# A price for changing the division of the PE array in a kernel's instruction planner

## The chip, the cores and the metric

One core of a Trainium2 chip runs the whole kernel. Its engines are TensorE (PE, the matrix engine with an array of 128 x 128), VectorE (DVE), ScalarE (ACT), GpSimd (POOL) and SyncE (SP, which issues most DMAs). The metric is the device time of one execution in microseconds. Before the change three runs took 1368.52 us in the median (1365.78 to 1373.71).

## The reference

One inference step of a network of two layers, width 1024, on 384 tokens: 128 context tokens and 256 latent tokens with caches of 128 more. Weights are shared by both groups of tokens; all data is float32. A layer is, in the reference's words cut to what matters:

```python
h = rmsnorm(x, norm1_g) * (1 + sc1) + sh1      # sh, sc, g of six: silu(c) @ w_mod + b_mod
z = split_cols(h @ w_in)                       # inputs of A, B, C, D and four gates
oa = gqa_attention(aq, ak_all, av_all)         # A: 4 heads of 64, q/k norm, rotary
ob = gla_bidir(bq, bk, bv, lg_f, lg_b, ...)    # B: gated linear attention, both ways, key width 32
oc = diff_attention(cq, ck_all, cv_all, lam)   # C: 4 heads, two softmaxes of width 32 subtracted
od = gqa_attention(dq, dk_full, dv_all)        # D: low-rank keys and values, 4 heads of 96
x = x + g1 * (sum(sigmoid(gate_j) * (o_j @ w_branch_j)) @ w_out)
h = rmsnorm(x, norm2_g) * (1 + sc2) + sh2
x = x + g2 * ((gelu(conv3(h @ w_ffu)) * (h @ w_ffg)) @ w_ffd)
```

After two layers there is a last norm, and the context tokens' keys, values and states of every layer are outputs too.

## The kernel before

**Dense work.** A weight tile of 128 rows comes by DMA into one of three raw buffers, is cast on ACT into a high part (wh), and DVE subtracts to get the low part (wl); there are three buffers of each. Activations are kept in two parts as well (hh, hl; act_h, act_l), and each product is three matmuls in float32r: high by high, high by low, low by high. This is the stream called main: it walks through 260 weight tiles in a fixed order. In a layer these are the inputs of A and D (zA, zD), of C (zC, zV), of B (bqk, zB); then for each of the branches A, D, C, B eight tiles of gate and branch projection; then the output projection, the FFN's up projection (function ffn_up and the ones before it) and its down projection (ffn_down: eight output tiles of three weight tiles each, 66 matmuls of 384 columns).

**Small work.** Four mixers run beside main as streams of their own (mixer_a to mixer_d), and so does the modulation of later phases (mods): DVE multiplies a row of w_mod by the conditioning value and adds it to an accumulator, 8 rows for each half of a group and for 2 conditioning vectors; finish (line 450) then sums over the partitions with a list of eight matmuls that have 32 weight columns, transposes, and adds the bias. The next half waits until finish's list has been issued. Groups (layer, which of six): (0,2), (0,3), (0,4) in the mixers of layer 0; (0,5), (1,0), (1,1), (1,2) in its FFN; (1,3), (1,4) in the mixers of layer 1; (1,5) in its FFN. A group has two halves. The residual after the down projection of layer 0 (resid, line 1368) holds its PSUM bank until (0,5), (1,1) and (1,0) are done.

**The planner.** All streams are Python generators, and the class Sched merges them into the engines' programs when the kernel is built. It keeps an estimated clock for each engine (self.t), made of prices for each instruction (Op.price; a dense matmul of 384 columns counts 163 ns). In each step run() takes, of all streams that offer an instruction or a list of instructions, the one with the smallest rank: the start in whole ns, then the priority, then the order of creation.

```python
t = max(t, self.t[op.eng] + (1283.0 if self.swap(op) else 0.0))
...
return t // Q, s.prio(), s.seq
```

The first line is in start() (line 165) and is followed by the times at which inputs are ready and outputs free; the last is rank()'s (line 177). emit() (line 183) puts one instruction into its engine's program and moves the clock; every instruction of the kernel is issued in line 208, so the profile has that line throughout. Priorities (line 45): finish 0, A 1, D 2, C 4, B 6, the modulation's DVE work 6, main 9; the smaller wins. A stream that waits for a condition or a buffer offers nothing until it has it.

**Places where main waits.** For a weight tile (getw); for a PSUM bank of kind D (three of them, while the mixers have four of kind M and the modulation and the norms share one of kind X); in the last input tile of B (zB) for the end of A (line 1268); in the first tile of each branch (branch, line 1322) for the end of its mixer; at the end of a phase for the streams of that phase.

**Divisions of the array.** By rows used of the array and columns of weights, rounded up to 32, 64 or 128: dense matmuls, most transposes and the scores of C and D (96 rows) are 128 x 128. A's scores are 64 x 128 (64 rows), the value products of A and D and D's keys 128 x 64, B's gate inputs 64 x 128 (33 rows), B's far levels 32 x 128, B's near levels and finish 128 x 32.

Of the kernel before, what the change touches and what calls it, by code (L numbers as in the profile page):

```python
# [48 lines left out]
MS = (0, 5), (1, 0), (1, 1), (1, 2), (1, 3), (1, 4), (1, 5)  # L49
MG = ((0, 2), (0, 3), (0, 4)), MS[:MN[0]], MS[MN[0]:MN[1]], MS[MN[1]:]  # L50
TICK = 3413.0
WIN, THIN = 4500.0, 0.3
RC = (0.6127977038364543, -2.043313830363309, 1.8766171890415242)

# [2 lines left out]


class Op:
    """One instruction, made now and put into its engine's program later."""  # L60

    def __init__(self, eng, fn, f, args, kw):
        aps = [(k, v) for k, v in list(enumerate(args)) + list(kw.items()) if isinstance(v, bass.AP)]
        self.eng, self.fn, self.f, self.args, self.kw = eng, fn, f, args, kw
        self.outs = [v for k, v in aps if k in (0, "out", "accum_out")]
        self.ins = [v for k, v in aps if k not in (0, "out", "accum_out")]
        self.cost = self.price()
        self.func = TABLES.get(args[2]) if fn == "activation" else None
        self.rows = self.ins[0].shape[0] / 128 if eng == "P" else 0
        self.thin = self.rows == 0.25  # L70
        if self.rows and self.outs[0].free_size() == 2:
            self.rows = 0.02

# [33 lines left out]


class Slots:
    """Buffers of one kind, handed out and given back by the streams."""  # L110

    def __init__(self, sched, pool, tags, shape):
        self.sched, self.pool, self.free, self.shape = sched, pool, list(tags), shape
# [27 lines left out]


class Sched:
    """Merges streams of instructions into the engines' programs: of the streams' next instructions the one that can
    start first by the engines' estimated clocks is put in, ties by priority. A stream yields an instruction, a list
    of instructions that stay together, a condition to wait for, or a buffer it asks for."""

    LAT = dict(zip("PVS", LATS))

    def __init__(self):  # L150
        self.t = dict(P=0.0, V=0.0, S=0.0, G=0.0, D=0.0, Q=0.0)
        self.ready, self.touch, self.table = {}, {}, "none"
        self.live, self.seq, self.groups, self.thin = [], 0, Counter(), Counter()
        self.duty = Counter()

# [9 lines left out]
    def start(self, ops):  # L165
        t = 0.0
        for op in ops:
            t = max(t, self.t[op.eng] + (1283.0 if self.swap(op) else 0.0))
            for v in op.ins:
                t = max(t, self.ready.get(v.name, 0.0))  # L170
            for v in op.outs:
                for e, x in self.touch.get(v.name, {}).items():
                    if e != op.eng:
                        t = max(t, x)
        return t
# [7 lines left out]
    def emit(self, op):  # L183
        b = self.start([op])
        if op.eng == "P":
            i = b // TICK
            cost = op.cost * (1 if self.duty[i - 1] > 0.375 * TICK else 2)
            self.duty[i] += min(cost, (i + 1) * TICK - b) * op.rows
            self.duty[i + 1] += max(0.0, b + cost - (i + 1) * TICK) * op.rows
        else:  # L190
            cost = op.cost
        e = self.t[op.eng] = b + cost
        if self.swap(op):
            self.table = op.func[:2]
        if op.thin:
            self.thin[b // WIN] += cost
        if op.fn == "dma_start":
            n = op.outs[0]
            q = max(e + 650, self.t["Q"])
            e = self.t["Q"] = q + n.shape[0] * n.free_size() * 4 / 360.0  # L200
            d = e + 900
        else:
            d = e + self.LAT.get(op.eng, 130.0)
        for v in op.outs:
            self.ready[v.name] = d
        for v in op.ins + op.outs:
            self.touch.setdefault(v.name, {})[op.eng] = d
        op.f(*op.args, **op.kw)  # L208
# [46 lines left out]
def trunk_kernel(es, tc, a, o):  # L255
# [79 lines left out]
    def mm(out, lhsT, rhs, start, stop):  # L335
        return PE.matmul(out, lhsT=lhsT, rhs=rhs, start=start, stop=stop)
# [1 line left out]
    def tr(out, x):  # L338
        return PE.transpose(out, x, ident)

    # weights: load, split into two parts of float32r, use

    st = dict(dma=0, use=0, want=-1)
    ready = {}
# [71 lines left out]
        yield from prod()  # L416
        yield V.scalar_tensor_tensor(y, t, 1.5, y, op0=ALU.add, op1=ALU.mult)

    # modulation

    def mod_setup():
        cv = C("cvec").rearrange("p (k m) -> p k m", k=8)
# [65 lines left out]
        yield has(("acc",) + todo[-1][:3])  # L488
        pool.release(*acc)

    # norms

    def bcast(ph, y, want):
        b = yield X.ask()
# [146 lines left out]
            else:  # L641
                yield S.activation(dst[:, s:e], dst[:, s:e], AF.Identity, scale=scale, bias=sh[:, m:m + 1])

    # mixers

    def rope(z, h, n, cos, sin):
        half = n // 4
# [585 lines left out]
        done.difference_update([("acc", h) for h in range(4)])  # L1233
        done.add(("B", l))

    # dense parts

    def evac(env, name, t, p, bank, n, l):
        z = env[name]
# [236 lines left out]

        return [([(a["wfd%d" % i][l, d], 128 * FD[i])], lambda d=d, i=i: part(d, i)) for d in range(8) for i in range(len(FD))]

    # phases

    mx = fp = None

# [362 lines left out]
```

## Time and profile before

| | before |
|---|---|
| median of three runs | 1368.52 us |
| span of the profiled execution | 1371.2 us |
| PE busy | 1352.2 us, 8230 matmuls |
| DVE busy | 1025.2 us |
| ACT busy | 674.7 us |
| mean granted clock of PE | 0.988 |

The profile is one execution of its own, with a span from the first to the last instruction. Busy times are unions of instructions; matmuls are pipelined, so the duration that a row gives for one is longer than the distance to the next, and a distance is read from the starts. Names are those of tiles, out <- in, without buffer numbers: d, m and x are PSUM banks, mr and sq the modulation's buffers, kT, q, k, e of the attention mixers, pk, s, zD, rt of B.

### The profile page before, as it was taken

The page shows a single profiled execution, that of the slowest core. Times are in us where ns is not written, and L with a number is a line of the kernel's source. Part 1 is how long each engine was busy: PE and PEld are TensorE (multiplying, and loading weights), DVE is VectorE, ACT ScalarE, POOL GpSimd, SP SyncE. Part 2 cuts the span into 40 slices and gives each one's busy share as a digit, 9 for nine tenths or more (in the row PEclk, how much of TensorE's full clock was granted, in tenths as well). Part 3 has the DMA queues.
Part 4 walks back from the last instruction along what each step waited for, and adds up shares of the span by engine and source line. Part 5 has one row for each costly group of instructions (what it writes and reads, how often), then busy time and mean ns, then how long its engine had stood idle before and what let it go on. Part 6 is the DMA issues. An engine that isn't in the chain of part 4 may idle for free. (4 is left out here: it accounts for less than half of the span.)

```text
span 1371.2 us, 22142 instructions
## 1 busy us (share of the span) xinstructions
PE 1352.2 (99%) x8230; PEld 1249.9 (91%) x8230; DVE 1025.2 (75%) x2141; ACT 674.7 (49%) x1298; POOL 27.3 (2%) x55
## 2 busy tenths in 40 slices
PE   8999999999999999999999999999999999999996
PEld 5786799889999999999998668889999999999996
DVE  5699799876578999997479897786556889655433
ACT  4545665664366444433354566764344654444321
POOL 0000000100000000000001000100000000000000
PEclk8999999999999999999999998999999999999998
DMA  9754764223435566665447445222344365333331
GB/s 361 243 185 125 217 204 157 81 97 121 143 117 184 181 204 207 201 213 177 138 139 242 144 163 166 75 97 97 119 146 133 106 214 171 123 123 121 123 127 60
DMA packets 77084, 214.13 MB, mean 156 GB/s; under 512 B 9616, under 2 KB 17104, under 8 KB 76976
## 3 DMA queue, kind: packets, MB, share of 16 engines
q1 hardware_dynamic: 74592, 206.71, 45.9%
q0 software_dynamic: 2384, 6.00, 1.3%
q8 instruction: 65, 1.06, 0.3%
q14 instruction: 43, 0.35, 0.1%
HBM read 204.78 MB, written 7.90 MB: 155 GB/s over the span
## 5 line engine op out<-in xcount | busy, mean ns | idle before, releaser
L208 ACT CAST wh<-raw 128x1024 fp32r<-128x1024 f32 (+3 forms) x260 | 277.9, 1069 | 270.2 <-PE d L208 179.8
L208 PE MATMUL d<-hl,wh 128*128 128x384 f32 (+1 forms) x1184 | 405.4, 342 | 0.0
L208 PE MATMUL d<-hh,wl 128*128 128x384 f32 (+1 forms) x1184 | 405.4, 342 | 0.0
L208 PE MATMUL d<-hh,wh 128*128 128x384 f32 (+1 forms) x1184 | 401.7, 339 | 0.0
L208 DVE TENSOR_TENSOR wl<-raw,wh 128x1024 fp32r<-128x1024 f32 (+3 forms) x260 | 324.1, 1247 | 97.9 <-ACT wh L208 93.4
L208 PEld LDWEIGHTS d<-hh,wl 128*128 128x128 f32 x1184 | 223.6, 189 | 4.1 <-issue 3.6
L208 PEld LDWEIGHTS d<-hl,wh 128*128 128x128 f32 x1184 | 223.8, 189 | 3.4 <-issue 2.9
L208 PEld LDWEIGHTS d<-hh,wh 128*128 128x128 f32 x1184 | 223.6, 189 | 2.8 <-issue 2.4
L208 PE MATMUL d<-act_l,wh 128*128 128x384 f32 x352 | 119.4, 339 | 0.0
L208 PE MATMUL d<-act_h,wl 128*128 128x384 f32 x352 | 119.3, 339 | 0.0
L208 PE MATMUL d<-act_h,wh 128*128 128x384 f32 x352 | 119.2, 339 | 0.0
L208 DVE SCALAR_TENSOR_TENSOR sq<-sq,cact,sq 128x512 f32<-128x512 f32 x140 | 101.1, 743 | 3.5 <-DMA sq<-wmod_in 3.5
L208 DVE SCALAR_TENSOR_TENSOR mr<-mr,cact,mr 128x512 f32<-128x512 f32 x140 | 100.8, 744 | 1.9 <-DMA mr<-wmod_in 1.9
L208 ACT ACTIVATE gt<-d 128x384 f32<-128x384 f32 x64 | 31.4, 490 | 102.1 <-PE d L208 101.9
L208 DVE SCALAR_TENSOR_TENSOR fc<-d,vec,fc 128x255 f32<-128x255 f32 (+1 forms) x152 | 61.6, 411 | 26.4 <-ACT fc L208 25.7
L208 DVE SCALAR_TENSOR_TENSOR gt<-gt,d 128x384 f32<-128x384 f32 x48 | 26.6, 554 | 71.1 <-PE d L208 64.1
L208 PE MATMUL d<-wh,hh 128*128 128x512 f32 (+2 forms) x192 | 72.0, 375 | 1.0 <-DVE zC L208 1.0
L208 PE MATMUL d<-wh,hl 128*128 128x512 f32 (+2 forms) x192 | 70.9, 369 | 0.0
L208 PE MATMUL d<-wl,hh 128*128 128x512 f32 (+2 forms) x192 | 70.7, 368 | 0.0
L208 PEld LDWEIGHTS d<-act_l,wh 128*128 128x128 f32 x352 | 66.1, 188 | 0.3 <-issue 0.2
L208 PEld LDWEIGHTS d<-act_h,wl 128*128 128x128 f32 x352 | 66.1, 188 | 0.2 <-issue 0.2
L208 PEld LDWEIGHTS d<-act_h,wh 128*128 128x128 f32 x352 | 66.1, 188 | 0.2 <-issue 0.2
(321 smaller groups left out, 2076.5 us busy)
## 6 DMA issues: line engine op xcount, KB each, us to landing
raw<-wgb_in SPq DMA_DIRECT2D x64, 640.0 KB, 3.9
raw<-wf_in SPq DMA_DIRECT2D x72, 512.0 KB, 3.5
sq<-wmod_in SPq DMA_DIRECT2D x80, 256.0 KB, 3.3
mr<-wmod_in SPq DMA_DIRECT2D x80, 256.0 KB, 3.3
raw<-wfd_in SPq DMA_DIRECT2D x32, 448.0 KB, 3.3
raw<-wo_in SPq DMA_DIRECT2D x16, 512.0 KB, 3.5
raw<-wfd_in SPq DMA_DIRECT2D x16, 512.0 KB, 3.5
raw<-wf_in SPq DMA_DIRECT2D x16, 384.0 KB, 2.9
```

Of the source, the lines that this page charges most:

```text
L208: op.f(*op.args, **op.kw)
```

## The change

Each PE instruction gets a mode, the division of the array that it needs. The planner keeps the mode of the last PE instruction that it issued, and start() adds 95 ns for every PE instruction whose mode is another.

```diff
+SWITCH = 95.0
...
     def __init__(self, eng, fn, f, args, kw):
...
+        self.mode = tuple(32 if n <= 32 else 64 if n <= 64 else 128 for n in (self.ins[0].shape[0], self.ins[0].free_size())) if eng == "P" else None
...
     def __init__(self):
...
+        self.mode = (128, 128)
...
         for op in ops:
             t = max(t, self.t[op.eng] + (1283.0 if self.swap(op) else 0.0))
+            if op.eng == "P" and op.mode != self.mode:
+                t += SWITCH
...
     def emit(self, op):
         b = self.start([op])
         if op.eng == "P":
+            self.mode = op.mode
```

The first operand of a matmul is its weights (lhsT), so the mode is (rows, weight columns). Nothing else changes but comments: no instruction is added or taken away, only their order on the engines may be another.

## Rows read from the trace of the kernel before

**Rows 1.** The page: busy time of the engines; PE's granted clock in 40 slices

```profile
PE 1352.2 (99%) x8230; PEld 1249.9 (91%) x8230; DVE 1025.2 (75%) x2141; ACT 674.7 (49%) x1298; POOL 27.3 (2%) x55
...
PEclk8999999999999999999999998999999999999998
```

**Rows 2.** Waits of PE: who for whom, us in total, times, longest

```profile
PE m L208 <- DMA pk<-wmp_in: 3.8, 1, 3.8
...
PE d L208 <- DVE zC L208: 1.0, 3, 0.4
```

**Rows 3.** The page's costliest groups: busy, mean ns | idle before, releaser

```profile
L208 ACT CAST wh<-raw 128x1024 fp32r<-128x1024 f32 (+3 forms) x260 | 277.9, 1069 | 270.2 <-PE d L208 179.8
```

**Rows 4.** Timeline of PE around one small list: start, us, instruction

```profile
301.60 0.34 PE L208 MATMUL d<-hh,wh 128*128 128x384 f32 x1
301.87 0.43 PE L208 MATMUL m<-pk,s 128*32 128x128 f32 x8
302.23 0.44 PE L208 MATMUL d<-hh,wl 128*128 128x384 f32 x1
302.50 0.34 PE L208 MATMUL d<-hl,wh 128*128 128x384 f32 x1
302.68 0.33 PE L208 MATMUL d<-hh,wh 128*128 128x384 f32 x1
```

**Rows 5.** Timeline of PE: the first and the last small run of 119

```profile
11.11 1.08 PE L208 MATMUL m<-pk,oc 128*32 128x256 f32 x8 [3.80 <-DMA pk<-wmp_in]
...
1168.04 0.65 PE L208 MATMUL x<-mr,cst 128*32 128x128 f32 x16
```

**Rows 6.** Timeline of PE in the first FFN

```profile
473.50 0.64 PE L208 MATMUL x<-mr,cst 128*32 128x128 f32 x16
...
597.70 0.34 PE L208 MATMUL d<-act_h,wh 128*128 128x384 f32 x1
```

**Rows 7.** Stretches: length, busy PE, PEld, DVE, ACT, POOL, clock, DMA

```profile
249.00:329.00 80.00, 80.00 (x576) 71.25 (x575) 61.94 (x134) 49.34 (x110) 3.95 (x8) 1.00 0.26 90
...
416.00:597.00 181.00, 181.00 (x1097) 178.60 (x1096) 168.91 (x305) 84.64 (x129) 0.00 (x0) 1.00 0.62 199
```

**Rows 8.** Tile mr: durations min/median/max, first and last start

```profile
L208 DVE SCALAR_TENSOR_TENSOR mr<-mr,cact,mr x140: 736/745/752, 437.6 to 1166.3; 128x512 f32<-128x512 f32 x140
...
L208 DVE TENSOR_SCALAR mr<-mr,cact x20: 475/480/490, 436.1 to 1145.4; 128x512 f32<-128x512 f32 x20
```

**Rows 9.** Timeline of PE: A, then D, then B in layer 0

```profile
94.02 2.65 PE L208 MATMUL m<-kT,q 64*128 64x128 f32 x10
...
117.59 0.61 PE L208 MATMUL m<-e,zA 128*64 128x128 f32 x8
...
124.50 1.07 PE L208 MATMUL m<-kT,pk 128*64 128x512 f32 x2
...
155.29 0.88 PE L208 MATMUL m<-e,s 128*64 128x128 f32 x12
...
328.01 0.49 PE L208 MATMUL m<-cs,k 128*128 128x128 f32 x3
```

**Rows 10.** Same stretch, tile wh (PE, PEld, DVE, ACT), tile gt (DVE, ACT)

```profile
249.00:329.00 80.00, 59.31 (x219) 39.20 (x218) 16.36 (x11) 13.82 (x11) 1.00 0.26 90
...
249.00:329.00 80.00, 12.17 (x22) 5.34 (x11) 1.00 0.26 90
```

**Rows 11.** Stretches as in rows 7 with their clock; timeline of PE there

```profile
828.00:831.00 3.00, 2.36 (x7) 1.96 (x8) 2.86 (x5) 0.00 (x0) 0.00 (x0) 0.63 0.87 229
831.00:834.00 3.00, 3.00 (x8) 1.91 (x8) 0.11 (x1) 1.30 (x5) 0.00 (x0) 0.50 0.46 134
...
837.00:840.00 3.00, 3.00 (x13) 3.00 (x13) 2.46 (x6) 1.28 (x4) 0.00 (x0) 0.67 0.45 138
...
832.24 0.52 PE L208 MATMUL d<-hh,wh 128*128 128x384 f32 x1
832.55 0.52 PE L208 MATMUL d<-hh,wl 128*128 128x384 f32 x1
```

## The prediction

> **What bounds the kernel now.** I read the page's totals first: the matrix engine (PE) is busy for 1352 of 1371 us, at full clock in nearly every slice, with VectorE (DVE) at 75% [rows 1]. Then PE's waits: the largest is 3.8 us, the rest are smaller, and none is for a weight part (wh, wl) [rows 2]. ScalarE's casts of weights, on the contrary, wait for PE to give buffers back: of 270.2 us of idle time before them, 179.8 was ended by PE [rows 3]. So the dense stream, "main" of the plan, always has its next matmul ready, and the mixers' small work (attention, B's chunks, modulation) is squeezed between. The time is the sum of PE's work, as long as the small work is always done when main needs it.
>
> **What the change removes.** A small list put into dense work at 301.87 starts 0.27 us after the matmul before it; dense matmuls follow each other at 0.17 to 0.18; after the list the second dense matmul comes 0.27 after the first [rows 4]. So a change of division costs 0.27 - 0.175 = 0.095 us, each way. Going along PE's timeline I count 119 runs of small divisions between dense ones or transposes and 247 changes; the first and the last run stand in [rows 5]. All changes together: 247 x 0.095 = 23 us. That is the ceiling of the gain, 1.7%; half of it, 12 us, is what a good gathering could bring.
>
> **What the change does to the order.** The edit stands in start(), which rank() uses to compare streams. In 128x128 division a dense matmul that is ready starts at PE's clock, exactly. A small list of n matmuls is ranked at that clock plus n x 95 ns, because the price is added for every operation of the list while the mode stays as it is: 95 for one A score, 570 for a value product of six, 380 for a near list of B, 760 for the eight of a modulation's finish. Before, both had the same start and the mixers' better priority decided. Now main wins each comparison, matmul after matmul, until it has nothing to offer. Priority is the second key and no longer counts. So small lists wait for main to stop, and by [rows 2, 3] main does not stop on weights. It stops where it asks for a result: zB's last part for A, a branch's first part for its mixer, the down projection for a bank. Transposes and the 96-row scores of C and D have the 128x128 division and aren't held up.
>
> Now each place. Main's dense work runs past and then stands still; PE does the small work that it owes anyway, so the loss is the stand minus that work.
>
> **Modulation in the first FFN.** finish is the list of eight (16 matmuls in the trace) that ends each half of a modulation group, and the next half can't begin until it is issued, as it reuses the two accumulators. Eight such halves belong to this FFN. Before, the first finish came at 473.50, in the middle of the up projection; it slips in without main stopping [rows 6]. PE is busy for 181.00 of the 181 us from 416 to 597 [rows 7], so a finish priced at 760 ns finds no opening. It stays. The down projection begins at 597.70 [rows 6]; each of its eight tiles is 66 matmuls x 0.175 = 11.6 us; the residual of each keeps its bank (D has three) until the modulations (0,5), (1,1) and (1,0) are done, which are the first six halves. Tiles 0 to 2 run, then main asks for a fourth bank at about 597.7 + 34.7 = 632 and stops. Only then does finish 1 go, and five halves follow one after the other: each 2 x 0.48 + 14 x 0.745 = 11.4 us of DVE [rows 8], plus 0.65 for its finish [rows 6] and some 0.3 between the engines (an estimate), 12.3 us. 5 x 12.3 = 61.5, with 2.5 for the last finish's copy, transpose, sum and the residual (estimate): 64 us of an empty PE. Cover that is gone: in the trace DVE spread these halves over 200 us. Bounds: 0 if some pause of main lets each finish through, 75 if the hand-overs take three times my 0.3 and the DMAs of the next weights also show. I take 64. It is the surest term.
> The seventh half is done by DVE during tiles 3 to 7; its finish goes where main waits for the phase's end, and the eighth half then costs 12.3 + 1.5 = 14 us (0 to 16). The second FFN has two halves (last finish at 1168.04 [rows 5]): the second is exposed in the same way, 14 us (0 to 16).
>
> **Mixer B, once per layer.** B starts after D with single gate matmuls (33 rows); before, they went while branch A was running, and B's last transposes went at 328.01 [rows 9]. Now the same event that frees B frees main, which runs through two branches without a stop, so B stands until main asks for it. Its heavy stretch is 249 to 329: DVE 61.94 less 16.36 of weights and 12.17 of merging is 33.4 us, ScalarE 49.34 - 13.82 - 5.34 = 30.2 us, PE 80 less 11 dense units of 30 x 0.175 is 22 us [rows 7, 10]; with the gates and cumulative sums before it about 38, 35 and 25. Engines overlap only in part: stand between 38 (DVE alone) and 74 (DVE and ScalarE in turn), I take 55, nearer a half overlap. Loss 55 - 25 = 30, twice 60 (bounds 0, if main pauses, to 98).
>
> **Mixers A and D.** A's scores started at 94.02 and its last value products at 117.59 [rows 9]; about 14 of these us are A's own PE work. Now the four M banks fill with waiting scores, D's transposes wait for banks as well, and main stops at the end of zB: some 19 us of stand, 5 lost. D's key products began at 124.50 and its last value products at 155.29 [rows 9], about 20 of it PE work: 27 of stand, 7 lost. Two layers: 24 us (0 to 50).
>
> **The rest.** Startup: its lists of four wait for the dense unit before them, but main soon wants their result: +2 (-2 to +8). The finishes of the mixer phases are done by DVE in B's stand: in the 55. Changes saved on PE's path: -5 (-12 to 0), since most of the gathering falls into stands where PE is not the limit. Clock: after gaps around 828 the granted clock was 0.63, 0.50 and 0.67 of full in three of the four stretches of 3 us up to 840, together about 10 us at the lower of the two levels, and dense matmuls followed each other at 0.31 to 0.32 [rows 11]: 10.2 x (1 - 0.175/0.32) = 4.6 us lost each time. Five long stands, of which I let half pay in full: 12 us (0 to 41).
> The Trainium skill (TensorE: Matmul & The Clock Gate, section Why this matters for your kernels) says that idle gaps between bursts of matmuls put the engine back to half rate. This speaks against any schedule that lets PE stand; [rows 11] agree for one gap, and by the rule all nine stands would pay, 41 us in place of 12, and the sum would be 29 us higher.
>
> Sum: 64 + 14 + 14 + 60 + 24 + 2 - 5 + 12 = 185. The profiled span of 1371.2 lies 2.7 above the median of the runs, 1368.5, and within their spread, so I forecast 1368.5 + 185 = 1554 us.
>
> **Rivals.**
> (a) Gathering works as described: main pauses often enough in the planner's own clocks that small lists go together in those pauses. For it: the planner prices a dense matmul at 163 ns where the trace has 175, so its PE is ahead of the real one and may see gaps that the trace doesn't. Half of the changes go: 1368.5 - 12 = 1357. Against: casts waiting for PE.
> (b) Main pauses at nearly every small list, and the order hardly moves: 1368, within 7.
> (c) Short lists (95 to 570) find openings where banks are evacuated, and the mixers keep their pace; only the finish at 760 starves. Then 64 + 14 + 14 + 2 - 5 + 4 (clock) = 93: 1462. It is decided by how long main waits for a bank at the changes of zC, zV, bqk and zB; in the trace PE waited 1.0 us for zC in three pieces [rows 2].
>
> **How the numbers follow.** Forecast 0.67, (c) 0.20, (a) 0.08, (b) 0.05. Half a per cent, 7 us, is about what can be told from no change here. Faster 0.08, same 0.05, slower 0.87. Range: from (c) with a shorter FFN wait, 1440, to the forecast with B and the clock near their upper bounds (+38 and +29, with +19 from the rest), 1640; it leaves out (a) and (b) and a little above.
>
> **What would show it.** In the new profile: no finish (x<-mr) between 440 and 600; then several at a pace near 12 us with PE idle and DVE running its multiply-adds; PE waiting some 180 us in all, mostly for DVE and ScalarE; B's near lists in one stretch without dense matmuls; small runs fewer and longer. If finishes still come one by one inside the up projection, the starving is wrong and (a) or (b) holds. If they are held but B's lists still lie between dense matmuls, it is (c).

## The result and the profile after

The changed kernel takes 1579.43 us in the median of four runs (1575.95 to 1581.07), the one before 1370.76 beside it: a ratio of 1.1515, interval 1.149 to 1.1541. It is 209 us slower; 185 were forecast. No instruction was added or taken away; only the order differs.

The page of the changed kernel, busy time by engine and PE's granted clock in 40 slices, answers [rows 1]:

```profile
PE 1390.7 (88%) x8230; PEld 1276.0 (81%) x8230; DVE 1039.9 (66%) x2141; ACT 677.3 (43%) x1298; POOL 27.0 (2%) x55
...
PEclk8999999966999999985997999999759999999988
```

PE now stands for 12% of the span, and its busy time has grown by 38 us with the same 8230 matmuls, because some of them run at the lower of the two clock levels (the slices marked 5 to 7). Its waits (who for whom, us in total, times, longest) answer [rows 2]:

```profile
PE x L214 <- DVE mr L214: 72.0, 7, 18.8
PE m L214 <- DVE rt L214: 22.0, 8, 5.5
PE m L214 <- DVE k L214: 14.3, 2, 7.1
PE m L214 <- DVE e L214: 11.3, 5, 3.9
```

The first row is the modulation (mr), the next three are nearly all B: seven waits of up to 18.8 us for DVE's accumulation, where before PE never waited for it. All of PE's idle gaps add up to 176 us, against 12 before.

In the first FFN no finish comes in the up projection. PE's timeline there, to be read beside [rows 6]; the down projection of this execution began at 657:

```profile
691.88 0.34 PE L214 MATMUL d<-act_l,wh 128*128 128x384 f32 x1
692.15 0.65 PE L214 MATMUL x<-mr,cst 128*32 128x128 f32 x16
...
703.36 1.23 PE L214 MATMUL x<-mr,cst 128*32 128x128 f32 x16 [9.62 <-DVE mr L214]
...
713.98 1.23 PE L214 MATMUL x<-mr,cst 128*32 128x128 f32 x16 [8.47 <-DVE mr L214]
...
750.11 0.69 PE L214 MATMUL d<-act_h,wh 128*128 128x384 f32 x1 [2.08 <-DVE xs L214]
```

Main's last matmul starts at 691.88, at the end of the third output tile, and its next at 750.11. In between come six finishes, the second 11.2 us after the first and the others 10.6 us apart, with DVE at its multiply-adds. Before branch B, beside [rows 9]:

```profile
318.52 0.34 PE L214 MATMUL d<-ol,wh 128*128 128x384 f32 x1
318.79 0.70 PE L214 MATMUL m<-pk,gT 33*128 33x256 f32 x2
...
327.03 2.90 PE L214 MATMUL m<-cst,rt 128*128 128x128 f32 x12 [5.45 <-DVE rt L214]
...
356.07 0.66 PE L214 MATMUL m<-rt,zD 128*32 128x128 f32 x8 [2.35 <-DVE rt L214]
...
391.91 1.51 PE L214 MATMUL m<-cs,k 128*128 128x128 f32 x6 [7.14 <-DVE k L214]
393.07 0.67 PE L214 MATMUL d<-hh,wh 128*128 128x384 f32 x1
```

The whole of B, from its first gate matmul to its last transposes, lies between two neighbouring dense matmuls, 74.6 us apart. Small work in general goes the same way. Of the 1150 matmuls of other divisions than 128 x 128, 558 lay before between two dense matmuls that start less than 1 us apart; now none does, and 988, against 92, lie between dense matmuls more than 8 us apart. Stretches with their busy time and clock (columns as in [rows 7]): B's, the one of the modulation, and the end of the first FFN.

```profile
319.00:393.00 74.00, 40.03 (x293) 25.98 (x293) 48.85 (x127) 41.07 (x107) 3.94 (x8) 0.60 0.09 30
...
681.00:750.00 69.00, 20.63 (x166) 14.48 (x164) 59.30 (x100) 4.97 (x10) 0.00 (x0) 0.61 0.62 187
...
820.00:845.00 25.00, 4.58 (x45) 2.70 (x45) 22.52 (x55) 8.11 (x20) 1.01 (x2) 0.62 0.25 79
```

**Where the 209 us went.** The two profiled executions differ by 203 us. I compare the start of each weight tile's first matmul in them. The lag of the changed kernel rises at few places: 5 us in the startup; 19.0 where main waits for A, 42.7 at D's branch and 73.8 at B's in layer 0, for the most part paid back, since the work of A, D and B that was put off no longer lies between the dense tiles (63 us are left when B is done); 58.0 in the down projection; 23.2 at the end of that phase; a net 48 in the mixers of layer 1; 14.6 in the second down projection. Each finish that is missing from an FFN gives back 0.9 us of dense time there. Changes of division fell from 247 to 161, which at 0.095 would be 8 us of gain.

### The profile page after: what moved, and what is told of

Its sections match the earlier page's. It is cut to its first block, busy times and chain, and to the rows that moved or that the text cites. A ratio compares the mean times of both kernels' runs of the same rounds, so it can differ in the third digit from the quotient of the medians.

```text
span 1574.2 us, 22228 instructions
## 1 busy us (share of the span) xinstructions
PE 1390.7 (88%) x8230; PEld 1276.0 (81%) x8230; DVE 1039.9 (66%) x2141; ACT 677.3 (43%) x1298; POOL 27.0 (2%) x55
## 4 chain that ended last, share of the span: by engine, by line
PE 79%; DVE 12%; ACT 3%; DMA 3%; issue 2%; SPq 0%; DVEq 0%; ACTq 0%
PE d L214 65%; PE m L214 13%; DVE mr L214 3%; DVE sq L214 2%; PE x L214 2%; DVE e L214 1%; DVE am L214 1%; DVE s L214 1%; DVE wl L214 1%; DMA sq<-wmod_in 1%; ACT rt L214 1%; DMA dk<-rt 1%; DVE k L214 1%; DVE sm L214 1%; DVE zD L214 0%
## 5 line engine op out<-in xcount | busy, mean ns | idle before, releaser
L214 DVE SCALAR_TENSOR_TENSOR mr<-mr,cact,mr 128x512 f32<-128x512 f32 x140 | 96.6, 745 | 0.6 <-DMA mr<-wmod_in 0.6
L214 PE MATMUL x<-mr,cst 128*32 128x128 f32 x160 | 10.5, 377 | 72.0 <-DVE mr L214 72.0
```

## The experiments

The theory (S): a list with a price in its rank waits until main stops, whatever its size, and the time is lost in those stands. Rivals: only lists with a large price starve (L); the new order loads the engines worse by itself (H).

**The price off the modulation's finish.**

```diff
         self.mode = ...
+        if eng == "P" and self.ins[1].free_size() == 128 and self.ins[0].free_size() == 32 and self.ins[0].name.startswith("cst"):
+            self.mode = (128, 128)
```

> The price stays on all small lists but the modulation's finish, whose mode is set to 128 x 128. Theory S (a priced list waits until main stops, and the loss is the sum of those stands): the three stands of the modulation (58 and 23 us in and after the first FFN, 15 in the second) go, finishes come one by one inside the up projection as before, the stands before branch B stay: about 1480, between 1460 and 1500. Rival L (only lists with a large price, 380 to 760, starve): finish is the longest list, so most goes: under 1430. Rival H (the loss comes from the new order's load on the engines, not from lists that wait): 1560 or more, since 20 of some 150 lists change.

1499.97 us, ratio 1.0934 (1.088 to 1.0988). S at its upper edge; L and H are out. The finishes of the first FFN are back inside the up projection (tile mr: durations, first and last start; the up projection ran from 480 to 671 here):

```profile
L216 PE MATMUL x<-mr,cst x160: 272/273/298, 546.5 to 1294.9; 128*32 128x128 f32 x160
```

and B's stands stay, 70.6 and 74.7 us between neighbouring dense matmuls.

**The price on finish alone** (the mode is set to 128 x 128 where the last two parts of that condition do not hold).

> The price is on the modulation's finish alone. Theory S: the FFN stands as in the changed kernel, 96 us; and with no stand before the branches any more, the finishes of the mixer phases find no opening there either, so the halves queue up at the output projection as they do at the down projection, at about 10.5 us each, some 30 us in each layer: 1370 + 96 + 60 = 1525, between 1500 and 1550. So the parts do not add: with the kernel above, they come to more than the whole. Rival L: 1370 + 96 = 1466 or less. Rival H: under 1400.

1535.14 us, 1.1191 (1.1135 to 1.1246), as S said, and the sum of both parts, 130 and 165, is more than the whole, 209. PE's waits show why:

```profile
PE x L216 <- DVE mr L216: 72.0, 7, 18.8
PE x L216 <- DVE sq L216: 60.4, 6, 11.2
```

The 72.0 of the FFNs (mr) are as in the changed kernel. The 60.4 (sq) are new: with no stand before the branches, the finishes of the mixer phases find no opening until the output projection asks for them. In the changed kernel B's stand hid these.

**A price of 1 ns** (SWITCH = 1.0).

> The price is 1 ns instead of 95, otherwise the changed kernel. Theory S: what matters is that main's start is PE's clock exactly, so any price above zero loses each comparison, whatever its size: most of the loss stays, 1530 to 1570; a little less than 1579, since openings of a few ns are enough now. Rival L: eight matmuls cost 8 ns, lists find openings everywhere: 1370 to 1385.

1559.13 us, 1.1365 (1.131 to 1.1421). With prices of 1 to 8 ns in the place of 95 to 760 the kernel loses 189 us in the place of 209. That settles L: the size hardly counts; main's rank is PE's clock to the nanosecond, so any price decides before priority can. Some openings do appear: PE's largest wait is smaller than above, 5 pieces in place of 7.

```profile
PE x L214 <- DVE mr L214: 53.9, 5, 18.8
```

**The price in the clock, not in the rank.**

```diff
-    def start(self, ops):
+    def start(self, ops, paid=0.0):
...
-                t += SWITCH
+                t += paid
...
-        b = self.start([op])
+        b = self.start([op], SWITCH)
```

> The price is counted when an instruction is issued, so the planner's clock of PE has it, but rank() compares starts without it. Theory S: priority decides ties again, nothing starves: 1370, within 7. Theory H: the clock is slower by 22 us than before and the planner's other decisions move with it: 1385 or more. If the count in the clock is worth something by itself: 1360 or less.

1378.63 us, 1.0049 (1.0025 to 1.0074). So nothing starves, and the comparison in rank() is what did the harm. It is 0.5% slower than before, more than S allowed: with 229 changes PE's idle gaps are 20 us against 12, in small waits such as these, the longest of them before D's scores:

```profile
PE m L214 <- ACT e L214: 3.5, 3, 2.7
PE m L214 <- DVE ol L214: 1.9, 1, 1.9
```

Why those grew I did not pursue.

**The price on B's small lists alone; on A's and D's alone.** The mode is set to (128, 128) for all others.

> The price is on B's small lists alone (gate inputs, far and near levels, and the transposes of 32 columns that feed the gates). Theory S with the sizes seen in the changed kernel: branch B's start is 73 us later relative to the tile before it in each layer, and about 25 of these are work that PE owed: 2 x 48 = 96 us, so 1466, between 1450 and 1485. With the prediction's size for B (30 per layer): 1430. Rival L: near and far lists (285 to 380) find openings: under 1400.

> The price is on A's scores, the value products of A and D, D's key products and the 64-row half of its query product. The prediction's size is 12 us per layer: 1394. From the changed kernel's stages it should be less: main's stands for A and D are long, but PE does owed work in most of them: 1375 to 1385.

B: 1481.59 us, 1.0789 (1.0748 to 1.083), 107 us; the forecast's 60 was too small. Its stands are 71.1 and 72.1 us. About 7 of the 107 for each layer may be D's: the 32-column transposes, priced here too, belong to a stream that D waits for, and main stands for some 35 us at D's branch. A and D: 1394.85, 1.0157 (1.0122 to 1.0192), 20 us; the prediction had 24, and what I expected from the stages of the changed kernel, 5 to 15, was wrong.

**B priced, with PE kept at work during B's stand.**

```diff
+        def warm(l):
+            p = yield D.ask()
+            while ("B", l) not in done:
+                yield mm(p[:, :NT], hh[0][:, :128], hh[0], True, True)
+            D.release(p)
...
             if k == 0 and i == 3:
+                spawn(warm(l), 8.5, "mx")
                 yield has((nm, l))
...
-        t = self.start(s.ops)
+        t = self.start(s.ops) + (500.0 if s.prio() == 8.5 else 0.0)
```

> As the version with the price on B's small lists alone (1481.6), but while main waits for B, PE is kept at work with throwaway matmuls of 384 columns into a free bank, put in where it would stand for 500 ns or more by the planner's clock (476 of them; they add work, no output uses them). It tells what lengthened the stand before branch B beyond the predicted 55 us. Theory K (the low clock during the stand, granted 0.60, slows B's own matmuls and so its chain): with the clock up, PE's owed work takes 25 us instead of 40 and the stand shrinks by most of the 15: 1450 to 1462. Theory E (B's chain alternates between DVE and ScalarE, which have no such clock, and PE is a small part of it): within 8 of 1481.

1468.72 us, 1.0688 (1.0666 to 1.0709): 13 less, between the two theories. Without and with the extra matmuls, B's stand in layer 0:

```profile
312.95:384.05 71.10, 36.15 (x263) 23.95 (x262) 38.68 (x107) 40.25 (x105) 3.94 (x8) 0.59 0.05 16
```

```profile
312.76:380.75 67.99, 66.82 (x497) 55.85 (x497) 39.66 (x109) 41.35 (x106) 3.97 (x8) 1.00 0.05 17
```

The clock went from 0.59 to 1.00, and the stands from 71.1 and 72.1 to 68.0 and 67.4. So the low clock holds 8 us of B's stands. By the starts in the two traces, the dense matmuls right behind them give back another 2.5. That is 10 of the 13; the rest is not placed, and the two runs without the extra matmuls lie 6 us apart. The 68 us that stay at full clock are B's chain itself. DVE and ScalarE do overlap in it: 39.7 us of DVE and 41.4 of ScalarE (the rows above), 21.1 of them at the same time by the starts and ends in the trace, which leaves 8.1 in which neither works. Which dependencies of B set this overlap I did not take apart.

**Gathering without starving.** Two versions in which a list of another division is ranked 95 ns later, once for the list, and only until it has been ready for a while (2000 or 1100 ns). The second also puts, among the mixers' lists that can start together, those of the present division first.

```diff
+HOLD = 2000
...
         t = self.start(s.ops)
+        op = s.ops[0]
+        if op.eng == "P" and op.mode != self.mode:
+            if s.since is None:
+                s.since = t
+            if self.t["P"] - s.since < HOLD:
+                t += 95
...
-        return t // Q, s.prio(), s.seq
+        p = s.prio()
+        if s.ops[0].eng == "P" and p < 9:
+            p = p / 10 + (s.ops[0].mode != self.mode)
+        return t // Q, p, s.seq
...
```

(The last four added lines are in the second version alone, with HOLD = 1100; in both, the price is in the planner's clock.)

> A version that gathers without starving: a list of another division is ranked 95 ns later, once for the whole list, and only until it has been ready for 2000 ns; the price is in the planner's clock. 186 changes of division instead of 247 in the order, and no stand. Theory S: 61 changes less at 0.093 us each is 5.7 us: 1364, if the mixers' delay of at most 2 us costs nothing; the version with the price in the clock alone lost 9, so 1364 to 1379. If gathering were worth more than its drains (fewer interruptions of the dense stream): 1355 or less.

> As the version with 2000 ns, but 1100 ns, and among the mixers' lists that can start at the same time those of the present division come first. 201 changes. Theory S: 46 less at 0.093 is 4.3 us: 1366, between 1364 and 1375.

2000 ns: 1374.92 us, ratio 1.0012 (0.9997 to 1.0028), no difference, though 61 changes are gone. 1100 ns: 1368.78 us against 1374.42 for the kernel before on the same chip, 0.9966 (0.9947 to 0.9985): a little faster, by 5.6 us, where 46 changes at 0.095 are worth 4.4. Its page and PE's largest waits:

```profile
PE 1340.9 (98%) x8230; PEld 1246.1 (91%) x8230; DVE 1026.4 (75%) x2141; ACT 672.7 (49%) x1298; POOL 27.1 (2%) x55
...
PEclk8999999999999999999999999999999999999998
```

```profile
PE m L224 <- DMA pk<-wmp_in: 3.5, 1, 3.5
PE m L224 <- DVE e L224: 2.7, 3, 1.3
```

PE's busy time is 11 us under that of [rows 1], while its idle gaps add up to 21 us against 12, in small pieces. With 2000 ns busy time is 9 us less and the idle gaps are 24 us, so the gain is lost again in waits: 6.5 us for C's keys, for instance.

```profile
PE m L221 <- DMA kT<-dk: 6.5, 2, 3.6
```

## Why the prediction was right

The mechanism held at each step that the runs could test. Main wins each comparison in 128 x 128 division: shown by the price of 1 ns and by the price in the clock alone. Small lists go only where main stops: shown by the counts of small matmuls above, and by the version in which finish alone is priced. Rivals (a) and (b) fell with the time, (c) with B's stands.

By terms:

- **Modulation in the first FFN: 64 forecast, 58.2 measured.** The place is right, the end of the third tile. The period is 10.6 and not 12.3, because DVE's multiply-adds start nearer to each other than the 0.745 that a row gives for one: 13 of them take 8.69, so 0.67 each. A duration was used where a distance was needed, the same trap that the prediction avoided for PE. DVE's timeline:

```profile
704.08 1.07 DVE L214 TENSOR_SCALAR mr<-mr,cact 128x512 f32<-128x512 f32 x2 [0.20 <-PE x L214]
...
705.80 8.69 DVE L214 SCALAR_TENSOR_TENSOR mr<-mr,cact,mr 128x512 f32<-128x512 f32 x13
...
714.69 1.07 DVE L214 TENSOR_SCALAR mr<-mr,cact 128x512 f32<-128x512 f32 x2 [0.20 <-PE x L214]
```

- **End of that phase: 14 forecast, 23 measured.** The eighth half shares DVE with other work: DVE is busy for 22.52 of the 25 us. **Second FFN: 14 forecast, 14.6 measured.**
- **B: 30 per layer forecast, about 49 measured** (stands of 74.6 and 73.3, less the 25 that PE owed). This is the term that was mis-sized. For the stand I took 55: 38 of DVE and 35 of ScalarE with 18 in common. The stand came out at the upper bound, 74, but not because the two worked in turn. With the price on B alone, the 71.1 us shown above are 38.7 of DVE and 40.2 of ScalarE, 19.2 of them in common, and 11.4 in which neither works, 10.4 of these with PE alone. So DVE's time and the overlap were right; ScalarE's time was 5 too small, and the forecast had no time for B's own matmuls on which both engines wait. It counted PE's part as owed work only, while it is also part of the chain, and the low clock lengthens it. In the changed kernel DVE's accumulations for one finish, 11.4 us, come into the stand as well.
- **A and D: 24 forecast, 20 measured** by themselves. A's stand in layer 0 is 19.2, as forecast; D's is about 41 in place of 27, but most of it is filled with owed work. What held D was not its key products first but the 64-row half of its query product, and the transposes of 32 columns.
- **Changes saved: 5 forecast, 8** by count. **Clock: 12 forecast** for the dense work behind five stands, about 7.6 measured (1.2 to 1.9 behind each, by the lag). What the forecast left out is the low clock inside the stands: the granted clock was 0.60 to 0.62 in the three stretches above, and B's two stands got 8 us shorter when it was kept up. Four of main's nine stands, those for A and D, stayed at 1.00, so 41 us for all nine was too much. **Startup: 2 forecast, 5 measured.**

So the sum was 24 us short. The terms above can't simply be added, since the measured stands hold the clock's cost and the saved changes too. Of the 203 us of the two traces, 5 lie in the startup, 105 in the mixers of both layers and 93 in the FFNs; the forecast had 2, 84 and 92, with 7 more for clock and changes. So what it missed lies in the mixers. That the FFNs agree to 1 us is in part luck: the wait at the down projection was forecast 6 too long, the end of the phase 9 too short.

## What to carry to other kernels

In a greedy planner that compares starts first and priorities second, a price on one kind of work is not a mild preference: if the other stream is always ready at the engine's clock, any price starves the priced work until that stream stops. Give such a price a limit in time, or let it break ties only, and look for the stream whose next step depends on the starved list. To size the stand that follows, follow the dependent chain through all of its engines, the waiting one's own steps included: the busiest engine's time, 38, and a half overlap of two engines, 55, were both too short for 74. And take distances between starts, not durations.

## What the runs showed of the hardware

- A change of the array's division costs 0.095 us each way in a dense stream at full clock (0.27 - 0.175, [rows 4]). A version with 46 of 247 taken away was 0.34% faster.
- PE's granted clock was 0.60 in a stand of 74 us, most of it at the lower level (1.2 GHz), although 293 small matmuls ran in it, 40 us of busy time. In B's stand with the price on B alone it was 0.59 over 71 us; with 234 more matmuls of 384 columns there it was 1.00.
